# A list scheduler inside the kernel, from the attention phase on, in place of the framework's instruction order

## The chip, the cores and the metric

One NeuronCore of one Trainium2 chip runs the whole program, in one launch. The metric is device time in microseconds (us); lower is better. Engines are named as in the profile: PE (matmuls; PEld is its weight load), DVE (vector), ACT (scalar), POOL (GpSimd), SP (it only issues DMAs here). Each engine works through its own list of instructions strictly in the order of that list and stops at an instruction whose inputs are not there yet.

## The reference, cut to what matters

One hybrid decoder layer on 2048 tokens of width 1024, all in float32:

```python
h = rms_norm(x, norm_g)
pa, pb, pc, pd, pm = split_cols(h @ w_in, GROUP_COLS)
ya = spatial_gating(...)         # A: gMLP over chunks of 128 positions
yb = forgetting_attention(...)   # B: causal attention with decay, 4 heads of 64
yc = mlstm(...)                  # C
yd = rwkv7_time_mix(...)         # D
ym = memory_attention(...)       # M: cross-attention into 256 memory tokens
mixed = concat([y * silu(z) for each branch])   # (1, 2048, 1280)
return x + mixed @ w_out
```

Matmuls of weights are made exact enough by splitting each float32 operand into a high part in the float32r type and a low rest, and by adding three products (high x high, high x low, low x high).

## The kernel before, in words

Tokens go in four blocks of 512. A projection of a token block onto 256 columns is a run of 48 or 96 matmuls (8 slices of the inner dimension, three products, two or four output tiles) into `pj` banks of PSUM (`proj_T`, `proj_T2`, `proj_tok`, `proj_tok2`; lines 256 to 320). Its weights are loaded by SP (`load_w`, L211), their high part is written by ACT (L222) and their low part by DVE (L225).

The program has three stretches. In the first (to about 942 us) groups D, M (last block), C and B are projected, and RWKV and mLSTM run beside them. In the second (942 to about 1470 us) groups A and M of the other blocks and the memory's keys and values are projected, and the attentions run beside them. In the third the output projection runs (L879, 960 matmuls), at first beside the last memory attentions.

The second stretch opens with `att.open()`. PSUM is then shared out as 2 `pj` banks, 3 `wk` banks, 2 `p2` banks (shown as `p`) and 1 `acc` bank. The attention is cut into 32 units (16 of forgetting attention `fu`, 16 of memory attention `mu`). A unit: loads of keys and queries by SP (L976, L989, L1002); splits by ACT and DVE (L994 to L1014); scores for the row maxima on PE into `wk` (L1026, L1028), reduced by DVE (L1040); the maxima turned by PE through `wk` (L1069) and put into the queries by ACT (L1070); scores again into `p2` (L1082 to L1085), exponentials by ACT (L1087), their sums by POOL (L1099, L1101), products with the values on PE into `acc` (L1108, tiles of 64 columns); at the end ACT and DVE take `acc` away (L1139, L1141, L1143), PE sums over partitions into `wk` (L1149), and the quotient goes through DRAM and back by four DMAs in a chain (L1159, L1163, L1167, L1171) to DVE (L1174).

What sets the order: Python generators are stepped in turns. After each slice of a projection `tick()` steps the weights, the evacuations (`evac`) and the lanes, each by its rate in `RATES` (fox=1.815). This gives the order in which instructions are written down. The framework's own scheduler then orders the instructions of each engine by a model of its own: those that were written earlier come first, but one that it thinks ready may pass one that it thinks late. An example in the trace is the constant copy L1063, which stands on ACT ahead of work written before it. Tiles are handed their buffers by that scheduler too.

Of the kernel before, what the change touches and what calls it, by code (L numbers as in the profile page):

```python
# [10 lines left out]
F32R = mybir.dt.float32r  # L11
# [4 lines left out]
PSUM = bass.MemoryType.PSUM  # L16
# [100 lines left out]
        yield from g  # L117


@with_exitstack  # L120
def body(ctx: ExitStack, tc, x, xT, mem, memT, wp, wkv, wout, pv, wa, sguT, sgub, out, dbg=None):
    nc = tc.nc
    V, A, G, T, SY = nc.vector, nc.scalar, nc.gpsimd, nc.tensor, nc.sync

    cp = ctx.enter_context(tc.tile_pool(name="cp", bufs=1))
# [11 lines left out]


    ident = cp.tile([P, P], F32, name="ident")
    make_identity(nc, ident)  # L140
    pvt = cp.tile([P, NPV], F32, name="pvt")
    SY.dma_start(pvt, pv)

# [618 lines left out]
    for q in (NQ - 1, 0, 1, 2):  # L762
        tok = slice(q * Q, (q + 1) * Q)
        if q < NQ - 1:
            hts = got()
            group_M(q)
        if q == NQ - 1:
            while ahead and next(ahead[-1][2], ahead) is not ahead:
                pass
            while evac.all or any(l.q for l in lanes.values()):  # L770
                evac.tick()
                for l in lanes.values():
                    l.step()
            csp.close()
            rctx.close()
            psx.close()
            ps = psx.enter_context(tc.tile_pool(name="ps2", bufs=1, space=PSUM))
            nbank = {"pj": 2, "wk": 3, "p2": 2, "acc": 1}
            att.open()

            fu = [Unit(att, True, h, g) for h in range(NH) for g in range(NQ)]
            mu = [Unit(att, False, h, g) for g in range(NQ) for h in range(NH)]
            lanes["fox"].q.append(att.run(fu[:-1] + mu[:NH] + fu[-1:] + mu[NH:]))
            sp = cw.enter_context(tc.tile_pool(name="sp2", bufs=1))
            stage.update(pool=sp, bufs=2, lag=2)

            sgw = mp.tile([P, NH, P], F32, name="sgw")
            SY.dma_start(sgw, sguT)
            G.affine_select(sgw, sgw, pattern=[[0, NH], [1, P]], compare_op=ALU.is_ge, fill=0.0, base=0, channel_multiplier=-1)
            sgb = mp.tile([P, 2, 1, P], F32, name="sgb")  # L790
            for p in range(2):
                for h in range(2):
                    SY.dma_start(sgb[64 * h:64 * h + 64, p, 0, :], sgub[2 * p + h:2 * p + h + 1, :].to_broadcast([64, P]))
            V.tensor_scalar(sgb, sgb, 0.25, None, op0=ALU.mult)


        wt = W("Av")
        gv = sp.tile([P, 2, 512], F32, tag="gv", name="gv")
        for i in range(2):
            evac.add(gate_values(proj_tok(wt, hts, 2 * i), gv[:, i]), "gl")  # L800
        wt = W("Au")
        gu = []
        for p in range(2):
            gu.append(sp.tile([P, 512], F32, tag=f"gu{p}", name="gu"))
            evac.add(gelu2(proj_T(wt, p, hts), gu[p]), "gl")
        wt = W("Az")
        if q == NQ - 1:
            evac.add(mem_rstd(), "gl")
        pts = proj_T2(wt, hts, send(load_mem, "mem_g", NMEM) if q == NQ - 1 else reload(q + 1) if q != NQ - 2 else None)
        for p in range(2):  # L810
            evac.add(spatial(pts[p], gu[p], gv, p, mixd[0][p][:, tok]), "gl")
        if q == NQ - 1:
            hm = got()
            evac.add(mem_keys(proj_tok2(W(0), hm, None, 2)[0]), "yn")
            evac.add(mem_values(proj_tok2(W(1), hm, reload(0), 2)[0]), "gl")
    evac.drain()
    cw.close()


# [18 lines left out]
        fox.step()  # L838
    while att.done < NH * (NQ + 1):
        fox.step()  # L840
    att.c5.close()
    op = att.c4.enter_context(tc.tile_pool(name="op", bufs=2, side="right"))
    while len(wo) < NK:
# [4 lines left out]
    for q in range(NQ):  # L848
# [15 lines left out]
        for e in range(2):  # L864
            es = slice(e * 512, (e + 1) * 512)
            for i in range(4):
                if e == 0 and i == 1:
                    load_m(1)
                for _ in range(3):
                    if len(wo) < 2 * NK:  # L870
                        load_wo()
                r = slice(q * Q + i * P, q * Q + (i + 1) * P)
                xr = op.tile([P, 512], F32, tag="xr", bufs=4, name="xr")
                SY.dma_start(xr, x[r, es])
                po = bank("pj")
                n = 0
                for k in range(NK):
                    for a, b in ((0, 0), (0, 1), (1, 0)):
                        T.matmul(po, mts[i // 2, k][:, a, i % 2 * P:(i % 2 + 1) * P], wo[e * NK + k][:, b], start=n == 0, stop=n == 3 * NK - 1)  # L879
                        n += 1  # L880
                    if k % 3 == 2:
                        tick()
                V.tensor_tensor(xr, po, xr, op=ALU.add)
                evac.held -= 1
                nc.scalar.dma_start(out[r, es], xr)
    att.close()


# [866 lines left out]
```

## Time and profile before

| | |
|---|---|
| timed runs | median 1742.38 us of 3 (1736.52 to 1743.93) |
| profiled execution | 1736.49 us, span 1734.8 us |
| mean granted TensorE clock | 0.975 of full |
| PE busy over the span | 1641.8 us (95%) |
| DVE, ACT, POOL busy | 1196.9 (69%), 881.3 (51%), 302.3 us (17%) |

Busy time is the time in which an engine had at least one instruction under way. A wait is the idle time of an engine just before an instruction, put down to whatever ended it. The granted clock of a stretch is a mean of its two levels, 1.2 and 2.4 GHz: 0.95 means that a tenth of the stretch ran at the lower one.

### The profile page before, as it was taken

The numbers are of one execution on the slowest core, as the hardware profiler recorded it, in microseconds if no ns is written. First come the engines' busy times: TensorE is split into PE (matmuls) and PEld (weight loads), VectorE is DVE, ScalarE is ACT, GpSimd is POOL, SyncE is SP. The second block draws the span as 40 slices with busy tenths as digits, with TensorE's granted clock in tenths as the row PEclk, the third lists the DMA queues.
The fourth block names the chain that finished last, engine by engine and source line by source line (L and its number), as shares of the span: only waits on it lengthen the run. The fifth ranks groups of instructions, "written<-read, shape, count | busy, mean of one in ns | idle before, by whom it ended". The sixth has DMA issues, their size and how long they took to land.

```text
span 1734.8 us, 31669 instructions
## 1 busy us (share of the span) xinstructions
PE 1641.8 (95%) x11306; PEld 1282.2 (74%) x11306; DVE 1196.9 (69%) x2990; ACT 881.3 (51%) x1895; POOL 302.3 (17%) x356
## 2 busy tenths in 40 slices
PE   7898999799999999999999999999999988999999
PEld 5676778687978888798888766667656655677887
DVE  7678685685977679488676887788687786752220
ACT  5566554544555455555444756566465646631110
POOL 5010000010100101010000045344444242100000
PEclk9999999899999999999999989999999999999999
DMA  6878654542453443344334544334334425654441
GB/s 198 256 230 259 184 161 97 139 145 86 135 157 101 132 141 115 86 134 146 98 101 141 167 120 130 105 102 130 96 86 110 113 68 137 191 162 114 143 130 56
DMA packets 200151, 234.36 MB, mean 135 GB/s; under 512 B 75016, under 2 KB 107336, under 8 KB 199992
## 3 DMA queue, kind: packets, MB, share of 16 engines
q1 hardware_dynamic: 185144, 218.69, 43.7%
q10 hardware_dynamic: 14848, 13.64, 2.6%
q8 instruction: 89, 1.46, 0.4%
q14 instruction: 70, 0.57, 0.1%
HBM read 180.44 MB, written 51.81 MB: 134 GB/s over the span
## 4 chain that ended last, share of the span: by engine, by line
PE 64%; DVE 16%; DMA 11%; ACT 4%; issue 3%; POOL 1%; SPq 1%; ACTq 0%; DVEq 0%; POOLq 0%
PE pj L315 14%; PE pj L879 12%; PE pj L267 12%; PE acc L1108 4%; DMA wraw<-in_wp 4%; PE pj L289 4%; DVE wt L225 2%; PE wk L1026 2%; PE p L1082 2%; PE p L1085 2%; PE rw L1359 1%; PE rw L1482 1%; PE rw L1484 1%; DVE ht L330 1%; DVE mx L1040 1%
## 5 line engine op out<-in xcount | busy, mean ns | idle before, releaser
L267 PE MATMUL pj<-ht,wt 128*128 128x512 f32 x1632 | 422.6, 403 | 5.8 <-DVE ht L330 2.7
L267 PEld LDWEIGHTS pj<-ht,wt 128*128 128x128 f32 x1632 | 298.3, 190 | 84.5 <-issue 10.5
L315 PE MATMUL pj<-wt,ht 128*128 128x256 f32 x2400 | 332.7, 290 | 9.3 <-ACT wt L222 3.4
L315 PEld LDWEIGHTS pj<-wt,ht 128*128 128x128 f32 x2400 | 304.9, 193 | 27.5 <-issue 7.4
L225 DVE TENSOR_TENSOR wt<-wraw,wt 128x512 fp32r<-128x512 f32 (+1 forms) x312 | 217.6, 700 | 78.0 <-ACT wt L222 76.4
L222 ACT CAST wt<-wraw 128x512 fp32r<-128x512 f32 (+1 forms) x312 | 184.8, 601 | 140.2 <-DMA wraw<-in_wp 92.5
L879 PE MATMUL pj<-wo,mt 128*128 128x512 f32 x960 | 231.3, 398 | 1.8 <-ACT wo L830 1.8
L879 PEld LDWEIGHTS pj<-wo,mt 128*128 128x128 f32 x960 | 180.2, 189 | 47.2 <-issue 2.4
L1101 POOL TENSOR_TENSOR es<-es,pe 128x512 f32<-128x512 f32 (+3 forms) x128 | 153.7, 1201 | 103.9 <-ACT pe L1087 98.9
L289 PE MATMUL pj<-ht,wt 128*128 128x512 f32 x480 | 138.9, 426 | 13.3 <-ACT wt L222 11.7
L1087 ACT ACTIVATE pe<-p 128x512 f32<-128x512 f32 x192 | 100.3, 541 | 50.3 <-PE p L1085 43.9
L1040 DVE TENSOR_REDUCE mx<-wk 128x1 f32<-128x512 f32 (+3 forms) x192 | 111.8, 614 | 18.2 <-PE wk L1026 14.3
L289 PEld LDWEIGHTS pj<-ht,wt 128*128 128x128 f32 x480 | 91.8, 200 | 39.1 <-ACT wt L222 12.1
L1108 PE MATMUL acc<-pe,v 128*64 128x512 f32 (+3 forms) x384 | 104.0, 594 | 6.3 <-DVE at L1141 6.3
L329 ACT ACTIVATE ht<-xr,pvt 128x512 fp32r<-128x512 f32 (+1 forms) x88 | 61.4, 703 | 61.9 <-DMA xr<-hbd 29.2
L1099 POOL TENSOR_TENSOR es<-pe 128x512 f32<-128x512 f32 (+1 forms) x32 | 43.2, 1351 | 246.3 <-ACT pe L1087 200.3
L1026 PE MATMUL wk<-ka,qb 66*128 66x512 f32 (+3 forms) x224 | 73.2, 383 | 10.2 <-DVE mx L1040 9.7
L1082 PE MATMUL p<-qa,kb 128*128 128x512 f32 x192 | 75.8, 396 | 5.8 <-ACT pe L1087 5.8
L330 DVE SCALAR_TENSOR_TENSOR ht<-xr,pvt,ht 128x512 fp32r<-128x512 f32 (+1 forms) x88 | 68.4, 784 | 16.8 <-ACT ht L329 16.1
L859 ACT CAST mt<-mr 128x256 fp32r<-128x256 f32 x80 | 31.6, 406 | 94.1 <-DMA mr<-mix 50.3
L1026 PEld LDWEIGHTS wk<-ka,qb 66*128 66x128 f32 x224 | 41.0, 196 | 49.3 <-DVE mx L1040 19.5
L1085 PE MATMUL p<-qb,ka 68*128 68x512 f32 x192 | 75.4, 395 | 0.0
(332 smaller groups left out, 2423.1 us busy)
## 6 DMA issues: line engine op xcount, KB each, us to landing
wraw<-in_wp SPq DMA_DIRECT2D x288, 256.0 KB
xr<-hbd SPq DMA_DIRECT2D x56, 256.0 KB
mr<-mix SPq DMA_DIRECT2D x80, 128.0 KB
xr<-in_x SPq DMA_DIRECT2D x32, 256.0 KB
out<-xr ACTq DMA_DIRECT2D x32, 256.0 KB
xt<-in_x SPq DMA_DIRECT2D x24, 256.0 KB
xr<-in_xT SPq DMA_DIRECT2D x24, 256.0 KB
hbd<-xr SPq DMA_DIRECT2D x24, 256.0 KB
```

Source lines behind the costliest of these rows:

```text
L222: A.copy(wt[:, :, 0, :ncol], raw[:, :, :ncol])
L225: V.tensor_tensor(lo, raw[:, :, :ncol], wt[:, :, 0, :ncol].bitcast(F32), op=ALU.subtract)
L267: T.matmul(pt, wt[k // 2][:, k % 2, a, m * P:(m + 1) * P], hts[k][:, b, :], start=n == 0, stop=n == 3 * KT - 1)
L289: T.matmul(pts[m], wt[k // 2][:, k % 2, a, m * P:(m + 1) * P], hts[k][:, b, :], start=k + n == 0, stop=k == KT - 1 and n == 2)
L315: T.matmul(pt[:, ii * 256:ii * 256 + 256], hts[k][:, a, (i + ii) * P:(i + ii + 1) * P], wt[k // 2][:, k % 2, b, :], start=n == 0, stop=n = ...
L879: T.matmul(po, mts[i // 2, k][:, a, i % 2 * P:(i % 2 + 1) * P], wo[e * NK + k][:, b], start=n == 0, stop=n == 3 * NK - 1)
L1026: T.matmul(p1, self.qb[0:66, i * P:(i + 1) * P], self.k[kk][0][0:66, :w], start=True, stop=True, skip_group_check=diag)
L1040: V.tensor_reduce(*late.pop(), axis=AX.X, op=ALU.max)
L1082: T.matmul(p2[:, f:], kb[:, ks], self.qa[:, f:], start=True, stop=False)
L1085: T.matmul(p2[:, f:], ka[:, ks], self.qb[:, f:], start=False, stop=True)
L1101: G.tensor_tensor(self.sum[:, f:], self.sum[:, f:], e[:, f:], op=ALU.add)
L1108: self.att.nc.tensor.matmul(self.acc[64 * i:64 * i + 64, f:], self.v[:, kt], e[:, f:], start=kt < 2, stop=True, skip_group_check=True)
```

## The change: what it does

`nc` in `body` becomes a `Recorder`. Until `rec.start()` it passes every instruction straight on and only keeps the accesses. From `rec.start()`, called just before `att.open()`, it keeps each instruction in a list, with those that it depends on (found from the boxes of the tiles read and written), and issues nothing. `tc.manual_schedule()` turns off the framework's own ordering from there on. At three places `rec.flush()` sorts and issues what has been kept: after the last projection's evacuations, after the forgetting attentions are over, and at the end. No arithmetic, tile, buffer count or DMA is added or removed.

The sorter keeps a clock for each engine. At each step it takes, over all engines, the instruction that could start first; among those of one start the one recorded first. The cut diff:

```diff
+    SEM = 250.0
+    def price(self, o):
+        if o.fn == "dma_start":
...
+            each = 9 + min(last * 4, 2048) * 0.037
+            o.cost, o.lag, o.key = 460.0, 2400.0, packets * each / 11
+            return
+        if e == "tensor":
...
+            if lhs.dtype == F32R:
+                c = max(n / 2.4 + 16, 60.0)
+            else:
+                c = 2 * max(n / 1.2 + 5, cols / 1.2 + 5) * (0.55 if min(q) < 128 else 1.0)
...
+            o.cost, o.mode, o.lag = c, tuple(q), 200.0
+            return
...
+        if e == "vector":
+            if o.fn in ("tensor_tensor", "scalar_tensor_tensor", "tensor_reduce"):
+                o.cost = 160 + 1.12 * n
...
+            o.cost = max(o.cost, 215.0)
+        elif e == "scalar":
+            o.cost = (180 if ps else 220) + 0.835 * n
+            if isinstance(k.get("scale"), bass.AP) or isinstance(k.get("bias"), bass.AP):
+                o.cost += 85
+        else:
+            o.cost = 220 + {"tensor_tensor": 2.5, "memset": 0.7}.get(o.fn, 1.2) * n
+        o.lag = 30.0
+    def flush(self):
...
+        while left:
+            best = None
+            for e, lst in cand.items():
+                if not lst:
+                    continue
+                c = self.pick(e, lst, first)
+                if c and (best is None or c[:2] < best[:2]):
+                    best = c
+            start, _, o = best
+            cand[o.eng].remove(o)
+            self.place(o, start, live)
+            order.append(o)
...
+        for o in order:
+            getattr(getattr(self.nc, o.eng), o.fn)(*o.a, **o.k)
+    def after(self, p, o):
+        if p.eng == o.eng and p.fn != "dma_start":
+            return 0.0
+        return p.done + (self.SEM if o.fn != "dma_start" else 3 * self.SEM)
+    def room(self, o, first):
...
+            if self.turn[tag][0] != t.name:
+                return None
+            if not s:
+                return None
+            at = max(at, min(s))
+        return at
+    def pick(self, e, lst, first):
...
+            s = max(clk, o.ready, r + self.SEM if r else 0.0)
+            n = o.rank
+            if e == "tensor" and self.mode not in (None, FULL):
+                if o.mode != FULL and o.mode == self.mode and s <= clk + 60:
+                    n -= 1 << 30
+                elif o.mode != FULL and s <= clk + 60:
+                    n -= 1 << 29
+            c = (s, n, o)
...
+    def place(self, o, start, live):
...
+            if self.mode is not None and o.mode != self.mode:
+                cost += 190.0 if o.mode == FULL else 150.0 if self.mode == FULL else 100.0
...
 def body(ctx: ExitStack, tc, x, xT, mem, memT, wp, wkv, wout, pv, wa, sguT, sgub, out, dbg=None):
-    nc = tc.nc
+    nc = rec = Recorder(tc.nc, tc)
...
             nbank = {"pj": 2, "wk": 3, "p2": 2, "acc": 1}
+            rec.start()
+            ctx.enter_context(tc.manual_schedule())
             att.open()
...
     evac.drain()
+    rec.flush()
     cw.close()
...
     while att.done < NH * (NQ + 1):
         fox.step()
+    rec.flush()
     att.c5.close()
...
                 nc.scalar.dma_start(out[r, es], xr)
+    rec.flush()
     att.close()
```

`turn` holds, for each tag, its tiles in recorded order: a buffer goes only to the tile whose turn it is. The mode of a PE instruction is the pair of array sizes (32, 64 or 128 rows and columns) that it uses.

## Rows read from the trace of the kernel before

**Rows 1.** Busy time by stretch: start and end, length, each engine (instructions), clock, DMA share, GB/s.

```profile
0.00:942.00 942.00, 891.49 (x7371) 740.30 (x7372) 692.86 (x2031) 494.62 (x1117) 91.85 (x176) 0.98 0.49 146
980.00:1480.00 500.00, 468.02 (x2602) 321.61 (x2602) 383.92 (x709) 298.56 (x592) 199.97 (x165) 0.95 0.41 112
1480.00:1595.00 115.00, 111.11 (x538) 80.42 (x537) 60.76 (x121) 46.06 (x98) 9.31 (x7) 1.00 0.58 161
1600.00:1735.00 135.00, 131.03 (x564) 105.88 (x562) 29.61 (x61) 15.51 (x39) 0.00 (x0) 0.99 0.35 109
```

**Rows 2.** Waits of PE, 942 to 1735 us: us in total, times, longest.

```profile
PE wk L1026 <- DVE mx L1040: 9.7, 10, 3.2
PE wk L1069 <- DVE mm L1020: 7.1, 5, 2.0
PE acc L1108 <- DVE at L1141: 6.3, 3, 4.5
PE p L1082 <- ACT pe L1087: 5.8, 5, 2.3
```

**Rows 3.** Timeline, stalls behind a DMA: start, us, instruction, idle before it.

```profile
1041.34 0.62 ACT L222 CAST wt<-wraw 128x512 fp32r<-128x512 f32 x1 [3.28 <-DMA wraw<-in_wp]
1042.51 0.50 PE L1082 MATMUL p<-qa,kb 128*128 128x512 f32 x1 [1.77 <-ACT pe L1087]
...
1269.61 0.62 ACT L222 CAST wt<-wraw 128x512 fp32r<-128x512 f32 x1 [4.62 <-DMA wraw<-in_wp]
1271.26 0.50 PE L1082 MATMUL p<-qa,kb 128*128 128x512 f32 x1 [2.31 <-ACT pe L1087]
...
1322.23 0.68 DVE L1174 TENSOR_TENSOR ao<-ao,at 64x512 f32<-64x512 f32 x1 [3.25 <-DMA ao<-dn]
1326.66 0.62 PE L315 MATMUL pj<-wt,ht 128*128 128x256 f32 x3 [2.98 <-DVE z L390]
...
1460.10 0.48 PE L1069 MATMUL wk<-identr,mm 128*4 128x128 f32 x4 [2.00 <-DVE mm L1020]
```

**Rows 4.** Timeline, stalls behind a lengthened DVE instruction beside POOL.

```profile
1000.17 2.82 POOL L1101 TENSOR_TENSOR es<-es,pe 128x512 f32<-128x512 f32 x2 [0.47 <-ACT pe L1087]
1000.25 1.23 DVE L155 SCALAR_TENSOR_TENSOR rq<-rq,ss 128x2 f32<-128x2 f32 x1
1003.67 0.47 PE L1026 MATMUL wk<-ka,qb 66*128 66x128 f32 x1 [3.22 <-DVE mx L1040]
...
1366.97 0.40 PE L1069 MATMUL wk<-identr,mm 128*4 128x128 f32 x4 [2.01 <-DVE mm L1020]
...
1414.34 3.68 PE L1108 MATMUL acc<-pe,v 128*64 128x512 f32 x8 [4.55 <-DVE at L1141]
```

**Rows 5.** Busy time of DVE on L154 alone, by stretch (instructions), clock, DMA share, GB/s.

```profile
0.00:942.00 942.00, 25.27 (x138) 0.98 0.49 146
942.00:1460.00 518.00, 19.46 (x48) 0.96 0.43 117
```

**Rows 6.** Busy time by slices of 20 us, columns as in rows 1.

```profile
1000.00:1020.00 20.00, 16.78 (x68) 11.19 (x68) 14.67 (x26) 7.96 (x17) 8.70 (x8) 0.66 0.36 98
1180.00:1200.00 20.00, 19.93 (x146) 15.26 (x145) 16.05 (x24) 11.65 (x23) 10.25 (x10) 1.00 0.60 157
1400.00:1420.00 20.00, 15.45 (x86) 9.21 (x84) 17.56 (x36) 10.77 (x22) 10.06 (x7) 0.83 0.29 82
```

**Rows 7.** Groups, 942 to 1735 us: busy us, mean ns of one, idle before.

```profile
L225 DVE TENSOR_TENSOR wt<-wraw,wt 128x512 fp32r<-128x512 f32 x77 | 62.8, 818 | 22.4 <-ACT wt L222 21.9
L1040 DVE TENSOR_REDUCE mx<-wk 128x1 f32<-128x512 f32 x112 | 73.9, 680 | 7.8 <-PE wk L1026 7.1 <-PE wk L1028 0.5
L1087 ACT ACTIVATE pe<-p 128x512 f32<-128x512 f32 x144 | 82.7, 595 | 42.3 <-PE p L1085 36.1 <-POOL es L1101 4.1 <-PE acc L1108 0.7
L859 ACT CAST mt<-mr 128x256 fp32r<-128x256 f32 x80 | 31.6, 406 | 94.1 <-DMA mr<-mix 50.3 <-DVE xr L883 28.9 <-PE pj L879 8.9
L860 DVE TENSOR_TENSOR mt<-mr,mt 128x256 fp32r<-128x256 f32 x80 | 32.8, 421 | 38.7 <-ACT mt L859 38.4
```

**Rows 8.** Timeline around the start of the output projection.

```profile
1451.67 0.40 ACT L859 CAST mt<-mr 128x256 fp32r<-128x256 f32 x1 [0.73 <-DMA mr<-mix]
...
1471.39 1.51 SPq L732 DMA_DIRECT2D mix<-mo  x2
...
1476.67 2.81 PE L879 MATMUL pj<-wo,mt 128*128 128x512 f32 x6
...
1492.18 0.50 PE L879 MATMUL pj<-wo,mt 128*128 128x512 f32 x1 [1.79 <-ACT wo L830]
```

236 lines of the change are left out of this document (235 added, 1 removed).

## The prediction, made before the changed kernel was run

> **What bounds the kernel now.** I read the busy time by stretch first. Up to 942 us nothing is changed except that instructions pass through the recorder, so those 942 us stand. From 1600 us PE is busy 131.0 of 135 us at a clock of 0.99 [rows 1], and the rest is the way out of the last result; nothing can be gained there by order alone. What the change can move lies between 942 and 1600 us. In 980 to 1480 us PE is busy 468.0 of 500 us, and in 1480 to 1595 us 111.1 of 115; DVE, the next busiest, is at 383.9 of 500 [rows 1]. So PE bounds this stretch, and its cost above pure PE work is 32.0 + 3.9 = 35.9 us of idle time.
>
> The granted clock comes on top. In 980 to 1480 us it is 0.95 [rows 1], between the levels of 1.0 (2.4 GHz) and 0.5 (1.2 GHz): 0.05 / 0.5 of 500 us, 50 us, ran at the lower one. Work done in them at half speed is 25 us lost at most (rounding of the clock makes it 22 to 28). The clock goes with the idle time: the slice with 16.8 of 20 us busy has 0.66, that with 15.5 has 0.83, one with 19.9 has 1.00 [rows 6].
>
> Then the waits of PE: the four largest kinds sum to 28.9 us, and three of them, 23.1 us, end with a DVE instruction [rows 2]. The timeline says why the releaser was late, and there are two kinds. In the first, ACT or DVE stands at an instruction whose DMA has not landed, and what PE wants is queued behind it: ACT waits 3.28 and 4.62 us for weights at L222 while the exponentials L1087 stand behind, and PE loses 1.77 and 2.31 us; DVE waits 3.25 us for `ao`, and PE loses 2.98; the stall of 2.00 us at 1460 is again behind L1174 [rows 3]. That makes 9.1 us. In the second kind a DVE instruction is long because POOL adds beside it: a 128x2 product of 1.23 us starts 0.08 us after a POOL sum, the reduction behind it is late, and PE loses 3.22 us; the stalls of 2.01 and 4.55 us have the same look around them [rows 4]. That makes 9.8 us. In all of these the projections' matmuls stood further back in PE's list.
>
> **The change, part by part.** Instructions, bytes and buffers stay, so only idle time, clock and seams count.
>
> *Recording up to att.open.* Issued at once and in the same order: 0.
>
> *Prices of the new sorter against rows.* A DVE tensor_tensor or reduction of 512 is priced at 160 + 1.12 x 512 = 733 ns; measured means are 818 (L225) and 680 (L1040). An exponential is priced at 607 ns, measured 595 [rows 7]. A 256 KB weight load is priced at 0.46 + 2.4 + 1.09 us (256 packets x 46.9 ns / 11) and 0.25 for the signal, 4.2 us; ACT stood 3.3 and 4.6 us at such loads [rows 3]. So a late DMA is now foreseen, and ACT and PE are given other work in its place. I let four fifths of the first kind go. As the first kind is 9.1 of the 18.9 us that I looked at, I take 48% of 35.9 = 17.2 us for it, and the gain is 13.8 us (bounds 0 and 17.2).
>
> *What the prices do not know.* A small DVE product such as L154 takes 25.27 / 138 = 183 ns in the first stretch, where POOL is busy 91.9 of 942 us, and 19.46 / 48 = 405 ns from 942 to 1460, where POOL is busy 200 of 500 us [rows 1, 5]. The price is 215 ns and nothing in it sees POOL. The second kind of stall is therefore not foreseen. Yet the list that PE works on is another one, and fuller of projections that are ready early; I let a third of the remaining 18.7 us go, 6.2 us (bounds: the 18.7 us double, to all of them gone, that is -18.7 to +18.7).
>
> The Trainium skill has a rule that speaks against this part (SBUF — State Buffer, section Who interferes with whom): a DVE instruction with two SBUF inputs and a GpSimd instruction that reads SBUF share a port pair, and whoever comes second waits until the first has finished. By that rule the 1.23 us above is POOL's, and no order that ignores POOL's clock can avoid it; the sum would then be 6.2 us worse, 4.3 more with the clock. The trace agrees: 183 against 405 ns.
>
> *Clock.* If 20.0 of 35.9 us of idle time go, I let the same share of the 25 us go: 14 us (bounds 0 and 25).
>
> *Grouping of small array modes.* Products L1108 and the sums of partitions may now be run together. There is no row of a larger group at full clock, so I take 0 (bounds: -4 to +8, a few tens of ns for each of 96 pairs).
>
> *The seams.* Nothing after a flush can pass what was issued before it. Before, the loads and splits of the output projection's operand (L859) ran from 1441 us on, beside the last projection, and L879 began at 1476.67 [rows 8]. These belong to the last flush now, and on SP they come after the last store of the spatial gating (1471.39 in this trace). Ten tiles have to be loaded and split before a first output is whole: on ACT 10 x 0.41 = 4.1 us, on DVE 10 x 0.42 = 4.2 us [rows 7], and the waits for DMA that are now hidden. Twelve memory units are still there as cover, but each is a chain. I charge 6 us (bounds 0 and 15). If the cover were gone altogether the ACT waits for `mr`, 50.3 us over 80 tiles [rows 7], give 6.3 us for ten tiles on top of the 4.2 us.
>
> *The wait that comes in.* Buffers of a tag go out in recorded order. In `wk` a tile whose producer is late, L1069 or L1149, holds back every score L1026 behind it, on PE and then on DVE. The framework's list had PE stop at such places as well (9.7 + 7.1 us, rows 2), so I charge nothing more; the upper bound is in the second rival.
>
> Sum against the profiled execution: 1736.5 - 13.8 - 6.2 - 14.0 + 6.0 = 1708.5 us. The timed median was 5.9 us above that execution and the lowest timed run equal to it; I add about half and predict 1711 us for the median.
>
> **The rivals.** *Order was not the limit (1735 us).* The unforeseen lengthening of DVE instructions only moves the stalls to other places: the first kind closes by a half (8.6 us), the clock by 5, the seam takes 6, the second kind grows by 3; net 5 us. For it: 23.1 us of PE's waits end with DVE, and DVE's excess stays. Against it: half of what I looked at began at a DMA. Into this case falls, too, that the new order is hardly another one, because among ready instructions both go by the order of writing.
>
> *The banks' turn (1754 us).* Head-of-line blocking in `wk`. Each of the 32 units has one L1069 and one L1149 in the turn, 64 in all. If each costs PE 0.4 us that neither `pj` nor `p2` work covers, that is 25.6 us of idle time, and with the 0.7 us that the clock lost for each idle us (25 / 35.9) 43.5 us. Against it stand the 34 us of gain less 6 at the seam: 15.5 us slower, 1752 against the profile and 1754 with the allowance. It decides from 28 / 1.7 / 64 = 0.26 us for each of the 64, where the gains are used up. For it: 16.8 us of PE's waits end at `wk` already [rows 2], and no tile may now pass a late one. Against it: `pj` has two banks of its own, and PE goes on with them while `wk` waits.
>
> *All gaps close (1684 us).* PE is never without a ready matmul until the seam: 35.9 + 25 - 6 = 55 us, or 1681.6 against the profile and 1684 with the allowance. For it: projections are nearly always there, and where PE is fully fed the clock is 1.00 [rows 6].
>
> **How the numbers follow.** I give the forecast (1695 to 1726) 0.42, all gaps close 0.22, order not the limit 0.19, the banks' turn 0.17. What a measurement can tell from no change is about 0.5%, 8.7 us, so faster means below 1733.7. Faster: 0.42 + 0.22 + a third of the third case, 0.06 = 0.70. Same: the rest of it, 0.13, and 0.02 of the last = 0.15. Slower: 0.15. The likeliest case alone has 1695 to 1726; with the bounds of the unforeseen stalls, the clock and the seam the range for 8 in 10 is 1680 to 1753.
>
> **What would show it.** Right: PE idle time in the stretch from att.open to the output projection's full run falls from about 36 to about 16 us, the clock there rises to 0.97 or 0.98, ACT no longer stands 3 us and more at L222 with exponentials behind it, and what stalls remain end with a DVE instruction that ran beside POOL. The seam shows as L859 starting only after the last `mix<-mo`, with PE idle or at the lower clock around the first L879. The first 942 us and the last 135 should be the same. Wrong: a PE idle time of 36 us or more with the waits moved from L1082 and L315 to L1026 and L1069 would speak for the banks' turn; the same idle time with the same DVE excess would say that order was not the limit.

## The result, and the profile after

| | before | after |
|---|---|---|
| timed runs, median | 1742.66 us of 4 (1736.52 to 1743.93) | 1718.44 us of 4 (1713.95 to 1721.73) |
| ratio, with its 95% interval | | 0.9879 [0.9849, 0.9909] |
| profiled execution | 1736.49 us, span 1734.8 us | 1720.24 us, span 1718.5 us |
| mean granted TensorE clock | 0.975 | 0.978 |

The change makes the kernel 1.2% faster. Ratios are of undisturbed runs; one run in six of the kernel e9 below took 7513.63 us and is left out. In the trace of the changed kernel every line label is L372 (the place that issues) or L234 (passed straight on), so instructions are told apart by their tiles. Busy time of each engine by stretch, after, with the columns of [rows 1]:

```profile
0.00:942.00 942.00, 891.10 (x7375) 739.40 (x7376) 694.01 (x2031) 495.74 (x1118) 90.40 (x178) 0.98 0.50 146
980.00:1480.00 500.00, 474.18 (x2692) 339.28 (x2690) 410.74 (x741) 311.89 (x615) 209.51 (x163) 0.96 0.44 119
1480.00:1595.00 115.00, 111.76 (x520) 82.65 (x521) 55.50 (x113) 37.19 (x85) 6.43 (x5) 0.97 0.58 159
1595.00:1718.00 123.00, 119.79 (x516) 96.80 (x514) 24.30 (x49) 11.91 (x31) 0.00 (x0) 1.00 0.32 101
...
1060.00:1080.00 20.00, 14.90 (x72) 9.70 (x72) 16.46 (x35) 10.29 (x19) 9.99 (x8) 0.98 0.32 82
...
1440.00:1460.00 20.00, 12.73 (x58) 6.66 (x55) 14.19 (x26) 10.51 (x23) 4.82 (x4) 0.70 0.82 218
...
1480.00:1500.00 20.00, 16.76 (x65) 10.59 (x66) 15.20 (x30) 11.90 (x26) 1.27 (x1) 0.83 0.90 241
```

The first 942 us are what they were (891.1 us of PE, 891.5 before). In 980 to 1480 us PE stands idle for 25.8 us in place of 32.0, and the clock is 0.96 in place of 0.95. That is a smaller change of both than the time suggests, because this stretch now holds two things of opposite sign. The worst slice is no longer in the middle: it is 1440 to 1460, just behind the end of the first list, with PE busy 12.7 of 20 us and a clock of 0.70.

Split at 1430 us, PE's idle time went from 28.5 to 18.6 us ahead of the seam, the place where the first list ends (942 to 1430, clock 0.96 to 0.98), and from 8.5 to 13.0 us around it (1430 to 1500, clock 0.93 to 0.85). Over all that follows 942 us, before and then after:

```profile
942.00:1735.00 793.00, 750.27 (x3936) 541.89 (x3934) 504.09 (x961) 386.68 (x779) 210.48 (x181) 0.97 0.44 122
942.00:1718.00 776.00, 741.24 (x3933) 547.57 (x3931) 514.05 (x959) 385.49 (x778) 220.29 (x178) 0.97 0.45 124
```

PE is busy for 9.0 us less, and up to its last matmul (at 1731.0 and 1714.8 us) it stands idle for 31.5 us in place of 38.8, which is 7.2 us less. So more than half of the 16.2 us is not idle time: the same matmuls take PE less time, in part by the clock.

What PE waited for after 942 us, after (us in total, times, longest):

```profile
PE p L372 <- ACT pe L372: 11.2, 7, 4.6
PE wk L372 <- DVE mx L372: 4.1, 4, 2.5
PE pj L372 <- ACT mt L372: 4.1, 4, 1.9
PE wk L372 <- ACT qb L372: 2.7, 1, 2.7
PE acc L372 <- DVE at L372: 1.7, 1, 1.7
PE wk L372 <- DVE mm L372: 1.2, 3, 0.6
```

Against [rows 2]: the waits that end with DVE fell from 23.1 us in three kinds to 7.0 us in the same three (`mx`, `mm`, `at`), and the wait for an exponential (`p` behind `pe`) rose from 5.8 to 11.2 us. The timeline shows what stands behind its longest case. Start, us, instruction, idle before it; after:

```profile
1068.02 3.42 POOL L372 TENSOR_TENSOR es<-es,pe 128x512 f32<-128x512 f32 x2 [0.58 <-ACT pe L372]
1068.51 1.77 DVE L372 TENSOR_TENSOR wt<-wraw,wt 128x512 fp32r<-128x512 f32 x1
...
1070.31 0.33 SPq L372 DMA_DIRECT2D wraw<-in_wp  x1
...
1072.99 1.09 SPq L372 DMA_DIRECT2D kr<-qk_Bk  x2
...
1073.54 0.62 ACT L372 CAST wt<-wraw 128x512 fp32r<-128x512 f32 x1 [4.41 <-DMA wraw<-in_wp]
...
1078.05 0.62 ACT L372 CAST ka<-kr 64x512 fp32r<-64x512 f32 x1 [3.89 <-DMA kr<-qk_Bk]
...
1079.09 1.07 ACT L372 ACTIVATE pe<-p 128x512 f32<-128x512 f32 x2
...
1079.73 0.80 PE L372 MATMUL p<-qa,kb 128*128 128x512 f32 x1 [4.57 <-ACT pe L372]
```

Read it from the end. PE waits 4.57 us for an exponential that ACT could have done earlier, but two casts stood ahead of it on ACT, and each waited for a load (4.41 and 3.89 us). This is the first kind of stall of the prediction [rows 3], still there. The load of 1070.31 was issued late: it left SP right behind a DVE product that reads such a buffer and took 1.77 us, beside two POOL sums. From 1072.99, when the first of two loads of keys was issued, to the cast are 5.1 us.

The second kind [rows 4] is still there as well, though rarer. Timeline, after:

```profile
1037.84 2.37 POOL L372 TENSOR_TENSOR es<-es,pe 128x512 f32<-128x512 f32 x2 [0.42 <-ACT pe L372]
...
1037.87 1.27 DVE L372 SCALAR_TENSOR_TENSOR rq<-rq 128x8 f32<-128x8 f32 x1
...
1041.53 0.69 PE L372 MATMUL wk<-ka,qb 66*128 66x512 f32 x1 [2.47 <-DVE mx L372]
```

And this is the seam, after:

```profile
1444.24 0.33 SPq L372 DMA_DIRECT2D mix<-mo  x1
...
1445.28 0.58 ACT L372 COPY at<-acc 64x512 f32<-64x512 f32 x1 [5.19 <-DVE ao L372]
...
1446.63 0.49 PE L372 MATMUL p<-qa,kb 128*128 128x512 f32 x1 [2.39 <-ACT pe L372]
...
1449.74 0.58 SPq L372 DMA_DIRECT2D mr<-mix  x1
...
1454.06 1.22 PE L372 MATMUL wk<-ka,qb 66*128 66x256 f32 x4 [2.73 <-ACT qb L372]
...
1455.91 0.71 ACT L372 CAST mt<-mr 128x256 fp32r<-128x256 f32 x2
...
1459.13 0.62 ACT L372 CAST wo<-wr 128x512 fp32r<-128x512 f32 x1 [2.51 <-DMA wr<-in_wout]
```

The last store of the spatial gating leaves SP at 1444.24, the first load of the output projection's operand at 1449.74, and its first split begins at 1455.91. ACT ends its first list with an idle time of 5.19 us. Before, `mr` was loaded and split from 1441 us on, beside the last projection [rows 8].

### The profile page after: what moved, and what is told of

Same layout as the page of the kernel before. It is cut to its first block, busy times and chain, and to the rows that moved or that the text cites. A ratio compares the mean times of both kernels' runs of the same rounds, so it can differ in the third digit from the quotient of the medians.

```text
span 1718.5 us, 31626 instructions
## 1 busy us (share of the span) xinstructions
PE 1632.3 (95%) x11306; PEld 1287.0 (75%) x11306; DVE 1208.1 (70%) x2990; ACT 881.2 (51%) x1895; POOL 310.7 (18%) x356
## 3 DMA queue, kind: packets, MB, share of 16 engines
q1 hardware_dynamic: 185144, 218.69, 44.4%
## 4 chain that ended last, share of the span: by engine, by line
PE 63%; DVE 18%; DMA 11%; issue 4%; ACT 3%; POOL 1%; SPq 1%; ACTq 0%; DVEq 0%; POOLq 0%
PE pj L372 22%; PE pj L234 20%; PE rw L234 6%; DMA wraw<-in_wp 4%; PE wk L234 4%; PE acc L372 4%; PE p L372 3%; PE wk L372 3%; DVE wt L234 2%; DVE rq L234 1%; DMA xr<-hbd 1%; DVE rq L372 1%; DMA xr<-in_xT 1%; DVE mx L372 1%; DVE wt L372 1%
## 5 line engine op out<-in xcount | busy, mean ns | idle before, releaser
L234 PE MATMUL pj<-ht,wt 128*128 128x512 f32 x1648 | 429.0, 407 | 19.0 <-ACT wt L234 13.9
L234 PEld LDWEIGHTS pj<-ht,wt 128*128 128x128 f32 x1648 | 304.2, 192 | 93.2 <-ACT wt L234 15.1
L234 PE MATMUL pj<-wt,ht 128*128 128x256 f32 x2016 | 274.5, 289 | 4.9 <-ACT wt L234 4.9
L234 PEld LDWEIGHTS pj<-wt,ht 128*128 128x128 f32 x2016 | 251.9, 192 | 12.2 <-ACT wt L234 5.3
L372 PE MATMUL pj<-wo,mt 128*128 128x512 f32 x960 | 234.4, 401 | 4.1 <-ACT mt L372 4.1
L372 PEld LDWEIGHTS pj<-wo,mt 128*128 128x128 f32 x960 | 181.7, 191 | 51.4 <-ACT mt L372 7.1
L234 DVE TENSOR_TENSOR wt<-wraw,wt 128x512 fp32r<-128x512 f32 (+1 forms) x236 | 156.9, 668 | 60.3 <-ACT wt L234 57.0
L234 ACT CAST wt<-wraw 128x512 fp32r<-128x512 f32 (+1 forms) x236 | 138.3, 595 | 105.8 <-DMA wraw<-in_wp 83.8
L372 POOL TENSOR_TENSOR es<-es,pe 128x512 f32<-128x512 f32 (+3 forms) x128 | 159.9, 1249 | 104.3 <-ACT pe L372 98.2
L372 PE MATMUL pj<-ht,wt 128*128 128x512 f32 x528 | 143.6, 401 | 3.0 <-DVE gv L372 2.9
L372 DVE TENSOR_REDUCE mx<-wk 128x1 f32<-128x512 f32 (+3 forms) x192 | 113.0, 616 | 39.8 <-PE wk L372 38.6
L372 ACT ACTIVATE pe<-p 128x512 f32<-128x512 f32 x192 | 100.6, 541 | 63.0 <-PE p L372 58.4
L372 PEld LDWEIGHTS pj<-ht,wt 128*128 128x128 f32 x528 | 95.6, 188 | 32.6 <-issue 12.0
L372 PE MATMUL pj<-wt,ht 128*128 128x256 f32 x768 | 110.4, 290 | 2.1 <-DVE gz L234 1.5
L372 PEld LDWEIGHTS pj<-wt,ht 128*128 128x128 f32 x768 | 102.6, 195 | 12.7 <-issue 5.5
L372 PE MATMUL acc<-pe,v 128*64 128x512 f32 (+3 forms) x384 | 103.4, 581 | 2.2 <-DVE at L372 1.7
L372 DVE TENSOR_TENSOR xr<-pj,xr 128x512 f32<-128x512 f32 x32 | 22.1, 690 | 98.0 <-PE pj L372 95.7
L372 POOL TENSOR_TENSOR es<-pe 128x512 f32<-128x512 f32 (+1 forms) x32 | 45.9, 1435 | 245.6 <-ACT pe L372 159.5
L372 ACT CAST mt<-mr 128x256 fp32r<-128x256 f32 x80 | 31.2, 405 | 113.1 <-DMA mr<-mix 47.0
L372 PE MATMUL p<-qa,kb 128*128 128x512 f32 x192 | 75.3, 397 | 11.2 <-ACT pe L372 11.2
L372 DVE TENSOR_TENSOR wt<-wraw,wt 128x512 fp32r<-128x512 f32 x76 | 67.3, 890 | 15.6 <-ACT wt L372 15.1
L372 PE MATMUL wk<-ka,qb 66*128 66x512 f32 (+3 forms) x224 | 70.7, 364 | 6.2 <-DVE mx L372 3.3
```

What stands on the lines that cost most here:

```text
L234: getattr(getattr(self.nc, eng), fn)(*a, **k)
L372: getattr(getattr(self.nc, o.eng), o.fn)(*o.a, **o.k)
```

## The experiments

Each was timed in five rounds against the kernel before on the same chip. Four chips were used (e0 to e3, e4 to e7, e8 to e10, e11), so kernels are compared by their ratios. PE's idle time and the clock are from one profiled execution, by stretch, so they can be compared with the split above. The fixed split fits kernels of about the same length. In e1 it cuts into a list that runs on to 2038 us; in e6 the last projection ends at 1417.8 us, so part of its seam is counted ahead of 1430.

| kernel | ratio to before, 95% | PE idle, 942 to 1430 | 1430 to 1500 | clock in the two |
|---|---|---|---|---|
| before | 1 | 28.5 | 8.5 | 0.96, 0.93 |
| e0, the change again | 0.9868 [0.9841, 0.9894] | 18.0 | 14.5 | 0.98, 0.88 |
| e1, recorded order | 1.1654 [1.1620, 1.1689] | 109.8 | 17.7 | 0.85, 0.83 |
| e2, DMA priced low | 1.0151 [1.0118, 1.0185] | 36.8 | 14.1 | 0.94, 0.89 |
| e3, ports known | 0.9925 [0.9900, 0.9949] | 22.3 | 14.4 | 0.99, 0.85 |
| e4, ports known, DVE alone priced | 0.9866 [0.9834, 0.9897] | 12.0 | 10.4 | 0.97, 0.83 |
| e5, landing 3.4 us | 0.9813 [0.9784, 0.9843] | 9.7 | 15.4 | 0.99, 0.83 |
| e6, no POOL sums | 0.9744 [0.9714, 0.9773] | 11.9 | 7.8 | 1.00, 0.89 |
| e7, four more flushes | 0.9919 [0.9891, 0.9947] | 20.3 | 18.7 | 0.99, 0.83 |
| e8, seam carried over | 0.9864 [0.9846, 0.9881] | 17.3 | 8.9 | 0.98, 0.88 |
| e9, e8 with e5 | 0.9832 [0.9814, 0.9850] | 9.9 | 14.6 | 0.99, 0.83 |
| e10, no grouping | 0.9912 [0.9895, 0.9929] | 13.7 | 8.8 | 0.99, 0.88 |
| e11, landing 4.4 us | 0.9917 [0.9889, 0.9946] | 19.0 | 16.5 | 0.97, 0.85 |

**e0. The changed kernel once more**, as the mark for the rest.

> The changed kernel again, as the base for the others on this chip: 1714 to 1722 us, 0.988 of the kernel before.

Measured: 1723.51 us, 0.9868. The gain repeats.

**e1. The order of recording in place of the sorter's.** Among the instructions that have their buffers, the one recorded first is taken, whatever its price; the preference for staying in an array mode goes too.

```diff
-                if c and (best is None or c[:2] < best[:2]):
+                if c and (best is None or c[1] < best[1]):
...
-            if e == "tensor" and self.mode not in (None, FULL):
+            if False:
...
-            if best is None or c[:2] < best[:2]:
+            if best is None or c[1] < best[1]:
```

> The recorder and the three flushes stay, but at each step the sorter takes the instruction that was recorded first among those that can be placed, not the one that can start first; its prices are without effect. Theory (the gain comes from passing late instructions by price): the gain is lost and more, because the framework's own passing is off as well: PE idle from 942 us on rises from 31 us (changed kernel) to 60 us or more, time 1750 us or more. Rival (the gain is from issuing in written order, undisturbed by the framework's wrong guesses): time stays within 6 us of the changed kernel's 1718.

Measured: 2037.08 us, 16.5% slower than before, far beyond what the theory had named; PE stands idle for some 262 us after 942 us, at a clock of 0.86. The waits of PE after 942 us:

```profile
PE wk L372 <- ACT qb L372: 164.8, 26, 17.3
PE p L372 <- ACT pe L372: 32.2, 13, 8.7
```

Scores stand on PE for queries that ACT has not put together, up to 17.3 us at a time. The generators' order relied on somebody to reorder it: before, the framework's model did, now the sorter does. So the sorting is what the change lives on, and the mere freezing of an order is not the gain. Grouping, which e1 leaves out as well, can't be behind this: alone it is worth 0.44% (e10).

**e2. A DMA priced as if it landed early.**

```diff
-            o.cost, o.lag, o.key = 460.0, 2400.0, packets * each / 11
+            o.cost, o.lag, o.key = 460.0, 400.0, packets * each / 11
...
-        return p.done + (self.SEM if o.fn != "dma_start" else 3 * self.SEM)
+        return p.done + self.SEM
```

> In the sorter alone a DMA's lag falls from 2400 to 400 ns and the extra two signals on waits of a DMA go. Theory (the price of a late DMA is a large part of the gain): ACT stands at weight casts more than in the changed kernel, PE idle rises from 31 to 40 us or more, time 1728 us or more. Rival (the order is insensitive to that price, since loads run behind their buffers anyway): time within 5 us of the changed kernel.

Measured: 1772.6 us, 1.5% slower than before and 2.9% slower than e0, as the theory had it. The waits of PE after 942 us show where the late loads come out:

```profile
PE p L372 <- ACT pe L372: 17.9, 11, 4.4
PE wk L372 <- DVE mm L372: 14.9, 9, 5.3
PE acc L372 <- ACT pe L372: 10.2, 6, 3.2
```

The time that a load is thought to take decides whether the sorter wins or loses. How much of the loss in e2 is due to the shorter landing and how much to the smaller allowance on what a DMA waits for is not separated; e5 and e11 move the landing alone.

**e5 and e11. A longer landing, 3.4 and 4.4 us.**

```diff
-            o.cost, o.lag, o.key = 460.0, 2400.0, packets * each / 11
+            o.cost, o.lag, o.key = 460.0, 3400.0, packets * each / 11
```

> The lag of a DMA in the sorter goes from 2400 to 3400 ns. Theory (loads still land later than priced, as with ACT standing 4.41 us at weights before PE's longest stall of 4.57 us): PE idle falls from 32 to 25 us or less, 0.982 or less of the kernel before. Rival (late loads are issued late, behind a lengthened DVE instruction that frees their buffer, and a longer lag doesn't model that): within 0.004 of the changed kernel's 0.9868.

> The sorter's allowance for a DMA's landing goes from 2.4 us (the changed kernel, 0.9868 of the time before) past 3.4 us (0.9813) to 4.4 us; nothing else. If loads that the sorter thinks there too early still leave stalls at 3.4 us, the gain goes on: below 0.980. If 3.4 us already covers what landings cost here, it stays: 0.980 to 0.984, with PE idle near the 25 us of the run at 3.4. If too long an allowance is itself a cost (work is put behind instructions that could have run, and loads are thought to be late at the seam), it comes back: 0.985 to 0.990.

Measured: 0.9813 at 3.4 us, the best kernel of this study, and 0.9917 at 4.4 us: e5's theory, and for e11 the last of its three cases, a little beyond the range given. Between 0.4 (e2, where the allowance for the signal was cut as well), 2.4, 3.4 and 4.4 us the ratio goes 1.015, 0.987, 0.981, 0.992: a curve with a floor. The intervals of e5 and e0 barely overlap, those of e5 and e11 are apart; e9 against e8, which differ by the same 1 us of landing, goes the same way (0.9832 against 0.9864). At 3.4 us PE's idle time ahead of the seam falls to 9.7 us, and the exponentials' waits shrink from 9.8 us (e0) to 1.1. The waits of PE at 3.4 us:

```profile
PE acc L372 <- DVE at L372: 7.8, 1, 7.8
PE p L372 <- ACT pe L372: 1.1, 2, 0.7
```

and at 4.4 us:

```profile
PE acc L372 <- DVE at L372: 9.4, 1, 9.4
PE p L372 <- ACT pe L372: 4.5, 6, 2.2
PE pj L372 <- DVE ht L372: 4.2, 2, 2.1
```

In both the longest wait is one single stall, 7.8 and 9.4 us, at the seam (1434 and 1442 us), where the first list has run out of projections and `acc` waits for its evacuation. With 4.4 us other work comes late too: projections now wait for `ht`, 4.2 us. A reading that fits, not one that was tested: a load that is thought later than it is makes the sorter put its users behind work that they should have passed.

**e3 and e4. A sorter that knows of POOL.** POOL instructions that read SBUF, and DVE instructions with two SBUF inputs (and its copies and scalings), exclude each other on the sorter's clock. e3 keeps the prices; e4 also lowers them towards what instructions take with nothing beside them.

```diff
+            if o.port:
+                s = max(s, self.port)
...
+        if o.port:
+            self.port = start + cost
```

and in e4 alone:

```diff
-                o.cost = 160 + 1.12 * n
+                o.cost = 150 + 1.04 * n
...
-            o.cost = max(o.cost, 215.0)
+            o.cost = max(o.cost, 180.0)
...
-            o.cost = 220 + {"tensor_tensor": 2.5, "memset": 0.7}.get(o.fn, 1.2) * n
+            o.cost = 220 + {"tensor_tensor": 2.07, "memset": 0.7}.get(o.fn, 1.2) * n
```

> The sorter learns that a DVE instruction with two SBUF inputs (and a DVE tensor_scalar or copy out of SBUF) and a POOL instruction that reads SBUF exclude each other: one clock more, prices unchanged. Theory (what is left of the idle time comes from DVE instructions lengthened beside POOL sums, directly or through buffers that are freed late and loads that then land late): PE idle falls from 31 to 22 us or less, DVE small products from about 0.4 us towards 0.2, time 1706 us or less. Rival (the rest is the seam at the output projection and chains of dependence): idle stays at 28 to 34, time within 5 us of the changed kernel.

> As in the run with the port clock, and the prices of DVE and POOL set to what the instructions take alone (a 512-column sum on POOL 1.28 us for 1.50, a DVE product of 512 0.68 for 0.73, a small one 0.18 for 0.215), since the old prices held a share of the lengthening already and were counted twice. Theory (double counting made the port clock a loss, 0.9925 of the kernel before against 0.9868): 0.983 or less of the kernel before, PE idle under 30 us. Rival (knowing of the lengthening is worth nothing, because a greedy sorter that waits for the port puts DVE work later as a whole): 0.988 to 0.996, PE idle 33 us or more.

Measured: 0.9925 and 0.9866; the second is the same as e0. Neither case of e3's expectation came: the time is 0.6% above e0, and PE's idle time over 942 to 1500 us is 36.7 us, against 32.4 in e0. PE's idle time did fall in e4, from 32.4 to 22.4 us over 942 to 1500 us, as its theory had it, but the clock fell with it (0.97 and 0.83 against 0.98 and 0.88; 51 us at the lower level after 942 us in place of 41), and the time did not follow. Why PE was granted less there is open. That e4 takes back the loss of e3 fits the reason given beforehand, that the old prices hold a share of the lengthening already; the lower prices without the exclusion were not run. Nor does the knowledge remove much of the lengthening. The products of 512 and of 8 elements (busy us, mean ns of one, idle before), 942 to 1500 us, in e4:

```profile
L377 DVE TENSOR_TENSOR wt<-wraw,wt 128x512 fp32r<-128x512 f32 x76 | 59.8, 789 | 10.3 <-ACT wt L377 8.5 <-PE wk L377 1.6
L377 DVE TENSOR_TENSOR rq<-rq 128x8 f32<-128x8 f32 x45 | 13.7, 305 | 1.5
```

**e6. No POOL sums.** The sums of the exponentials are left out, a constant stands in their place. This is no kernel to use; it shows what the sums cost the rest.

```diff
-                G.tensor_copy(self.sum[:, :f], self.first[:, :f])
-            G.tensor_tensor(self.sum[:, f:], self.first[:, f:], e[:, f:], op=ALU.add)
+            G.memset(self.sum, 1.0)
...
-                G.tensor_tensor(self.sum[:, f:], self.sum[:, f:], e[:, f:], op=ALU.add)
```

> The changed kernel without the sums of exponentials on POOL: a constant stands in for each unit's sum, so POOL reads nothing of them, all else is computed. Theory (POOL's sums lengthen DVE, and that is behind most of the stalls that are left before the output projection): DVE busy falls by 40 us or more, PE idle before the last flush from 19 to 8 us or less, time 1700 us or less. Rival (stalls come from chains and late loads whatever DVE takes): PE idle there stays over 14 us, time 1710 us or more.

Measured: 1698.29 us, 0.9744, 1.2% (some 22 us) below e0. Up to the end of the last projection PE stands idle for 7.8 us, in e0 for 18.0. The same products, 942 to 1500 us, without the sums:

```profile
L372 DVE TENSOR_TENSOR wt<-wraw,wt 128x512 fp32r<-128x512 f32 x76 | 53.0, 700 | 24.7 <-ACT wt L372 24.5
L372 DVE TENSOR_TENSOR rq<-rq 128x8 f32<-128x8 f32 x45 | 7.5, 166 | 1.5
```

and with them, in e0:

```profile
L372 DVE TENSOR_TENSOR wt<-wraw,wt 128x512 fp32r<-128x512 f32 x76 | 67.9, 897 | 15.6 <-ACT wt L372 15.1
L372 DVE TENSOR_TENSOR rq<-rq 128x8 f32<-128x8 f32 x45 | 14.4, 320 | 1.5
```

So 897 ns are 700 and 320 ns are 166 when POOL adds nothing. DVE's busy time in 980 to 1480 us falls from 409.6 to 358.3 us, and PE's idle time from 32.5 to 19.7 us (942 to 1500). The stalls beside POOL are real, and of what was tried on top of the change taking the sums out is worth most. The orders of e3 and e4 did not get at them. The other thing that e6 takes away, waiting for POOL itself, is small: from 942 to 1500 us all that waits for it in e0 is ACT, for a buffer, 1.1 us in total.

**e7 and e8. The seam.** e7 flushes at the end of each of the four token blocks as well. That makes three more seams ahead of the one that is there, and the fourth flush stands right before that one, with only the last evacuations between the two. e8 takes seams away: a flush goes on only until the last instruction that uses a closing buffer is issued, and what is left is kept and sorted again with the next part.

```diff
+        rec.flush()      (e7, at the end of a token block)
```

```diff
+        def due(o):
+            return pools is None or any(... in pools for t in o.tiles)
...
-        left = len(ops)
+        left = sum(due(o) for o in ops)
...
-        self.ops = []
+        self.ops = [o for o in ops if o.done is None]
```

> A flush more at the end of each of the four token blocks of the second stretch, so three more seams (the fourth falls on the one that is there). Theory (a seam costs what I charged, 6 us, since nothing later may fill the ends of the chains): 12 to 25 us slower than the changed kernel. Rival (seams are free, because the work on both sides is of the same kind and the engines carry their clocks over): within 5 us of it.

> The first flush now issues only up to the last instruction that uses a tile of the pools that close there, the second up to the last that uses the keys' pool; what is left over is kept and sorted again with the work of the next flush, so it can mix with it. Prices as in the change. Theory (the seam at the output projection, about 14 us of PE idle and the lower clock between 1430 and 1500 us, is the tail of DMA chains that nothing later may pass): idle in that stretch falls to 9 us or less, 0.982 or less of the kernel before (changed kernel 0.9868). Rival (the tail waits for stores, loads and buffers of the closing pools whatever the lists say): idle there stays at 13 to 16 us, 0.985 to 0.989.

Measured: 0.9919 in e7, which is 0.5% or some 9 us more than e0, between theory and rival (the intervals of the two barely overlap). PE's idle time grows by 2.3 us ahead of 1430, where the three new seams are, and by 4.2 us around the old one, where the fourth flush is (two executions of the change itself, after and e0, differ by 0.6 and 1.5 us in these columns); so the 9 us can't be put down to three seams of 3 us each. e8 has 0.9864 against 0.9868 for e0, no difference that can be told. Busy time around the seam, 1430 to 1500 us, e0:

```profile
1430.00:1500.00 70.00, 55.52 (x280) 35.77 (x276) 46.75 (x87) 42.80 (x90) 11.03 (x8) 0.88 0.69 184
```

and e8:

```profile
1430.00:1500.00 70.00, 61.07 (x309) 39.36 (x309) 54.20 (x101) 49.10 (x102) 13.23 (x9) 0.88 0.73 202
```

Carrying over gives PE 5.6 us of work more in these 70 us. In the profiled executions the span is 8.2 us shorter (1713.7 against 1721.9), in the ratios, which take out the difference of the chips, none of it is left. The seam costs idle time, that is shown; that carrying it over makes the kernel faster is not.

**e9. e8 and e5 together.**

> The carried seam and the DMA lag of 3400 ns together. Theory (the two act at different places, the lag before the seam, the carry at it): 0.976 or less of the kernel before. Rival (the longer lag already moved what the carry would fill, or the carry does nothing): 0.980 to 0.983, that of the longer lag alone.

Measured: 0.9832 [0.9814, 0.9850], not apart from e5 alone, as the rival had it. With the longer landing the idle time around the seam is back at 14.6 us, although work is carried over.

**e10. No grouping of array modes.**

```diff
-            if e == "tensor" and self.mode not in (None, FULL):
+            if False:
...
-                cost += 190.0 if o.mode == FULL else 150.0 if self.mode == FULL else 100.0
+                pass
```

> The sorter without array modes: no price for a change of mode and no preference for staying in one. Theory (grouping is worth nothing here, as I priced it): within 0.003 of the changed kernel's 0.9868. Rival (changes of mode cost PE, 190 or 150 ns each by the sorter's prices, and grouping is part of the gain): 0.990 or more, and PE's time per product pair longer.

Measured: 0.9912, 0.44% above e0, so the rival and not the theory, though PE's idle time is lower by 10.0 us (942 to 1500). Busy time of the products with the values alone (tile `acc`, columns as in rows 1 without POOL), 942 to 1430 us, e10:

```profile
942.00:1430.00 488.00, 98.07 (x340) 20.17 (x340) 13.11 (x21) 12.84 (x25) 0.99 0.42 117
```

and e0:

```profile
942.00:1430.00 488.00, 91.26 (x344) 25.38 (x344) 13.62 (x21) 12.87 (x25) 0.98 0.43 118
```

At nearly the same clock about as many matmuls take 6.8 us less when they follow one another in longer runs: after 942 us the 384 products stand in 71 runs in e0 and in 107 in e10, and PE's list changes its array mode 212 and 312 times. The matmul behind such a run is dearer as well. In the trace after, at the full clock, a projection matmul of 512 columns ends 430 ns after a product if it follows one (14 cases), and 231 ns after one of its own kind (437). PE is fuller in e10, but with dearer work.

## Why the prediction was right, and where its terms were not

The time came out at 1718 us where 1711 was predicted, inside the likeliest case's own range. The direction and its reason hold: the order in which ready work is offered to PE was worth about 1%, and it is the sorter's prices that bring it (e1, e2). The sum does not hold as well. It took 28.0 us off the profiled execution, whose span fell by 16.3, and more than half of these came out of PE's busy time (9.0 us), where the prediction had only the clock; idle time gave 7.2. Four of its signs did not come: over 942 to 1500 us PE's idle time went from 37.0 to 31.6 us and not to 16, the clock there stayed at 0.96, ACT still stood 4.41 us at weights with exponentials behind it, and the largest wait that is left, 11.2 us, ends with ACT and not with DVE. The first 942 us, the last stretch and the look of the seam were as foretold. Term by term:

- *Late loads, "I let four fifths of the first kind go", -13.8 us.* This step was too hopeful. PE's idle time ahead of the seam fell by 9.9 us for both kinds together (28.5 to 18.6), and the longest stall of the trace after is again of the first kind (1079.73). The text looked at whether a late DMA is foreseen at all; it did not ask whether the price of 4.2 us is long enough when loads are issued in a burst or when their buffer is freed late. At 3.4 us in place of 2.4 (e5) PE's idle time ahead of the seam falls by some 8 us more against e0, to 9.7. So the mechanism is the right one and the price was short.
- *Stalls beside POOL, -6.2 us.* The waits that end with DVE fell from 23.1 to 7.0 us, more than a third. But the lengthening itself stayed: small products take 320 ns, less than the 405 before [rows 5] but far from the 183 without much POOL work, and those of 512 elements 897 ns (both in e0; 818 before [rows 7]). Part of it may come back under another name, in loads that start late (1068.51 above). The Trainium skill's rule that the prediction weighed (SBUF — State Buffer, section Who interferes with whom) agrees with e6: with no POOL sums beside them the same DVE instructions take 166 and 700 ns.
- *Clock, -14.0 us.* Mis-sized. The time at the lower level fell only from 47.8 to 44.4 us, and PE's busy time in it from 44.1 to 39.3 us. Half of that is lost at half speed, 22.0 and 19.6 us: by this estimate 2.4 us were gained. Ahead of the seam the clock did what was forecast (0.96 to 0.98); around the seam it gave much of it back (0.93 to 0.85). The step failed where it let the clock follow the sum of idle time: 13.0 of the 31.5 us that are left are gathered in 70 us.
- *Seam, +6.0 us.* The look of it was as forecast, `mr` behind the last `mix<-mo` and the lower clock there. Its size is larger: 4.5 us of idle time, and of the 70 us some 11 more at the lower level, half of which are lost. That is about 10 us in the profiled execution. In time the four flushes of e7 cost some 9 us together; the seam of the change itself could not be measured in time by e8.
- *Grouping, 0 (bounds -4 to +8).* The sign was left open, and within the sorter it is a gain: taking the grouping away costs 0.44% (e10). Against the kernel before, the products themselves did not get cheaper. PE is busy with them (tile `acc`, the two rows below) for 104.0 and 103.4 us. But there are 212 changes of array mode in PE's list where there were 281, and one of the scores `wk<-ka,qb`, counted from the end of the matmul ahead of it, takes 211 ns on average in place of 247; that is 8.2 us over the 224 of them. Before, 31 of those at the full clock stood behind a product, after 14. So idle time (7.2 us) and clock (2.4) leave 6.6 us of the 16.2, and fewer changes of mode are the likely reason; no run separates them from the rest of the new order.
- *Recording to att.open, 0; the last stretch, 0.* Both hold: 891.1 against 891.5 us, and PE busy for 0.97 of its last 123 us as of its last 135 before.

Busy time of the products alone, columns as in rows 1 without POOL, before and then after:

```profile
942.00:1735.00 793.00, 104.00 (x384) 20.34 (x384) 21.06 (x32) 19.25 (x36) 0.97 0.44 122
942.00:1718.00 776.00, 103.43 (x384) 27.45 (x384) 21.07 (x32) 19.28 (x36) 0.97 0.45 124
```

The errors partly made up for each other: too much for loads and clock, nothing for what the matmuls themselves would save, and a seam that was too cheap. That 1718 lies so near 1711 is in part luck. Of the rivals, the turn of the banks did not show: the waits at `wk` for `mm` are 1.2 us. "Order was not the limit" is wrong as a whole, but what it named is a part that remains, for e6 finds 1.2% there.

What stays open: why the clock is lower in e4 although PE stands idle less, whether a seam carried over is worth time, and how the 6.6 us of PE's busy time divide.

## What to carry to other kernels

A list scheduler is as good as its price for what lands late: the allowance for a load was worth 3.4% of the whole time between its worst value (e2, with the smaller allowance for the signal) and its best, and it has an optimum, so it should be swept and not only set to a mean. Price the changes of array mode as well as the durations, and expect a list that ends (a flush, a phase) to collect the idle time that was removed from the middle. Where one engine lengthens another one's instructions, a sorter that knows of it need not help (e3, e4), while less work on the first one does (e6). Whether another engine could take the sums without giving the gain back was not tried.

## What the runs showed of the hardware

Two things were not expected. A DVE product of 512 elements that took 700 ns without POOL sums took 897 ns on average beside them, and single ones up to 1.77 us: not only the small instructions are lengthened. And PE's idle time alone does not tell the time of a variant: e10 is slower than e0 with 10.0 us less of it, for its matmuls take 12.7 us more (756.4 us against 743.7 after 942 us) with 312 changes of array mode in place of 212, and e4 is no faster with 10.0 us less, at a lower clock.
